# Two halves of an expert block's weighted sum moved earlier in a mixture-of-experts loop

## The chip, the cores and the metric

The kernel runs on one core of a Trainium2 chip. The metric is the device time of one execution in microseconds (us), as the median of several runs. TensorE (PE in the profile) multiplies matrices into PSUM, VectorE (DVE), ScalarE (ACT) and GpSimd (POOL) work element by element, SyncE (SP) issues the transfers from the chip's main memory, and each engine has an instruction queue of its own; semaphores tie them together.

## What is computed

A trunk of two layers over 256 tokens of width 1024. Each layer mixes tokens by three head groups side by side (windowed attention, a state space scan, latent attention) and then runs a mixture of 32 experts, of which each token takes two of one group of eight. The mixture is the part that matters here:

```
for g in range(N_EXPERT_GROUPS):
    h = silu(einsum('nd,edf->enf', xt, w_gate[g])) * einsum('nd,edf->enf', xt, w_up[g])
    h = h * gate[:, g].T[:, :, None]
    y = y + einsum('enf,efd->nd', h, w_down[g])
x = x + y
```

Every expert has three weight matrices of 1 MB (gate, up, down, each 1024 x 256 numbers of 4 bytes), so a layer's experts alone are 96 MB, which are read once.

## The kernel before

The function `moe` (L1194) walks over nine blocks per layer, seven of four experts and two of two. A block gives each of its experts an equal share of 128 slots: 32 with four experts, 64 with two. Its steps, with the names that the profile shows:

- **Weights.** All weights flow through a ring of 25 pages of 1 MB (tile `pg`). `pump` (L227) issues their transfers on SP in one fixed order; a page is taken again when the last instruction that reads it has run. Per block that is: first halves (`hf` 0) of gate and up of each expert, second halves (`hf` 1), then down.
- **Gather** (L1232, tile `gp`, copies into `xe`): one-hot matmuls pick the rows of the slots, in eight pieces k = 0 to 7. Two neighbouring blocks of four can share one gather. It is done one block ahead: the last block of such a group gathers for the next group, pieces 0 to 3 and then 4 to 7. The copies out of PSUM go to DVE and ACT in turn.
- **Gate and up** (`gate_up`, L1440, tile `gu`): 16 products per half with four experts, each recorded as two matmuls, 64 in all. In the last block of layer 1 the second half goes two experts at a time (L1447).
- **Hidden** (L1345): silu on ACT, a product on DVE. `hidden_t` (L1351, tile `hp`) turns it round on PE, and ACT copies it out.
- **Down** (L1459, tile `yp`): the product with the down weights; `split_y` (L1359) writes the sum as two parts, `yh` and `yl`.
- **Combine** (L1245, tiles `cp` and `x`): the block's sums go back to their tokens. It has two halves of 512 columns. One half is four matmuls (L1251, L1252: two for each 128 tokens) and two additions on DVE into `x` (L1253). It lies one block behind: the sums of a block (`pend`) are combined while the next block runs.

With four experts a slot share can overflow. Then a second pass runs under a condition that the chip evaluates: `tc.If(more > 0)` at L1568 (gather and first half of gate and up again) and at L1598 (second half, down and combine again). When it isn't needed, each engine waits there until its own earlier instructions are done, raises its semaphore by what it skips, and goes on. After one block of each layer (L1611) the pending sums are combined at once and the overflow of more than 64 tokens of an expert is handled (`units`, L1423); the block behind it has no `pend`.

The order in which a queue holds its instructions is not quite that of the source: the framework that lays the program out lets a later instruction pass one that is not ready by its own reckoning.

So in the source a block's order is: first half of gate and up, the condition of L1568, second half, hidden, [pieces 0 to 3 of the next gather], combine half 0, `hidden_t`, [pieces 4 to 7], combine half 1, the condition of L1598, down. The brackets are only in the last block of a gather group: blocks 0, 2, 3, 5, 7 of layer 0 and 0, 1, 2, 4, 5, 7 of layer 1, counted from 0.

Of the kernel before, what the change touches and what calls it, by code (L numbers as in the profile page):

```python
# [161 lines left out]
def hybrid_encoder_kernel(ctx, tc, I, out, dbg=None):  # L162
# [7 lines left out]
    def ps(name):  # L170
        return psp.tile([128, 512], F32, tag="ps", name=name)
# [83 lines left out]
    def page(*key):  # L255
        return st["tiles"][key]

    def done(*keys):
        for k in keys:
            del st["tiles"][k]  # L260
            st["ns"] -= 1
        pump()
# [931 lines left out]
    def moe(l, tab, rt):  # L1194
        with tc.tile_pool(name=f"moe{l}", bufs=1, reuse_waits="tile") as mo:
# [49 lines left out]
            def combine(pend, hfs=(0, 1)):  # L1245
                Sm, yh, yl = pend
                for hf in hfs:
                    for tt in range(2):
                        p = ps("cp")
                        c = slice(512 * hf, 512 * hf + 512)  # L1250
                        PE.matmul(p, Sm[:, 128 * tt:128 * tt + 128], yh[:, c], start=True, stop=False)  # L1251
                        PE.matmul(p, Sm[:, 128 * tt:128 * tt + 128], yl[:, c], start=False, stop=True)  # L1252
                        V.tensor_tensor(x[:, tt, c], p, x[:, tt, c], OP.add)  # L1253
# [186 lines left out]
            def gate_up(gu, blk, xs, hf, ahead=None):  # L1440

                m = 128 // len(blk)
                if ahead is not None:
                    for k in range(4 * hf, 4 * hf + 4):
                        ahead(k)

                two = end and blk == blks[-1] and hf == 1  # L1447
                for k, sp in [(k, s0) for s0 in range(0, len(blk), 2) for k in range(4 * hf, 4 * hf + 4)] if two else \
                        [(k, None) for k in range(4 * hf, 4 * hf + 4)]:
                    for s, e in list(enumerate(blk))[slice(sp, sp + 2) if two else slice(None)]:  # L1450
                        PE.matmul(gu[m * s:m * s + m, :].rearrange("p (a f) -> p a f", a=2), xs(k, s),  # L1451
                                  page(l, "gu", e, hf)[:, :, k % 4, :],
                                  start=(k == 0), stop=(k == 7), tile_position=(0, m * s))
# [51 lines left out]
            pend, scr = None, [None]  # L1505
# [8 lines left out]
            for g, grp in enumerate(groups):  # L1514
                if g < cut:
                    continue
                nb = len(grp)
                for ib, b in enumerate(grp):
                    blk, xe = blks[b], cur[1]
                    if b == UNIT_PREP[l] - 1:  # L1520
                        st["peak"] = 8
                    if b > 0:
                        scr[0] = work_page("scr")
                    if end and b == len(blks) - 1:
                        fin = [work_page(n) for n in ("fin", "yo")]
                        fg, xg = fin[0][:, :D], page_sm(fin[0], D, (2, 512))
                        yo = page_sm(fin[1], 0, (2, D))
                        nc.sync.dma_start(fg, I["final_g"].to_broadcast([128, D]))
                    if b == TAB_AT and tab is not None:
                        st["peak"] = 13  # L1530
                    m, o = 128 // len(blk), ib * len(blk)
                    if ib == nb - 1:
                        nxt = onehot(g + 1) if g + 1 < len(groups) else None
                        if nxt:
                            nxt[3](slice(0, 2))
                    gu, quad, w = ps("gu"), m == 32, {}
                    xs = lambda k, s: xe[:, k, o + s, :]
                    if b == 0:
                        ahead = lambda k: gather(cur[0], xe, k)
                        gate_up(gu, blk, xs, 0, ahead)  # L1540
                        if dbg and dbg.get("stop") == ("blk", l):
                            return
                        cn = counts()
                        if not quad:
                            done(*[(l, "gu", e, 0) for e in blk])
                        gate_up(gu, blk, xs, 1, ahead)
                        st["peak"] = 4
                        if not quad:
                            done(*[(l, "gu", e, 1) for e in blk])
                        scr[0] = work_page("scr")  # L1550
                        rt.gates()
                        pin(S.activation(mt([128, 1], "jka"), halfpi, AF.Silu))
                        uw["quad"] = quad_flags(cn)
                        pgt = weigh(cur[0], cur[2])
                    Sm, gs = fill_slots(slots([pgt[:, tt, o:o + len(blk), :].rearrange("p e c -> p (e c)")
                                               for tt in range(2)]))
                    if ib == nb - 1 and nxt:
                        pgt = weigh(nxt[0], nxt[2])
                    if quad:
                        if b > 0:  # L1560
                            gate_up(gu, blk, xs, 0)
                        f = blk[0] // 4
                        more = nc.values_load(uw["quad"][0:1, f:f + 1], min_val=0, max_val=1)
                        w = {"gu": ps("gu2"), "xs": page_sm(scr[0], 0, (8, 128)),
                             "P": scr[0][:, 1024:1280].rearrange("p (t e c) -> p t e c", t=2, e=4),
                             "S": slots(None, "2")[0]}
                        if b > 0:
                            with tc.If(more > 0):  # L1568
                                second(blk, w, 0)
                            done(*[(l, "gu", e, 0) for e in blk])  # L1570
                            gate_up(gu, blk, xs, 1)
                    elif b > 0:
                        for hf in range(2):
                            gate_up(gu, blk, xs, hf)
                            done(*[(l, "gu", e, hf) for e in blk])

                    hh = hidden(gu, gs)
                    for part in range(2):
                        if ib == nb - 1 and nxt:
                            for k in range(4 * part, 4 * part + 4):  # L1580
                                gather(nxt[0], nxt[1], k)
                        if pend is not None:
                            combine(pend, (part,))
                        if part == 0:
                            hT = hidden_t(hh)
                    if pend is not None:
                        work_done(1)
                    if b == 1:
                        uw["ui"], un = unit_list(cn)
                    y = w["y"] = y_page()  # L1590
                    if b == UNIT_PREP[l]:
                        unit_prepare()
                    if b == UNIT_AT[l]:
                        uw["y"] = y
                    if b > TAB_AT and tab is not None:
                        next(tab, None)
                    if quad:
                        with tc.If(more > 0):  # L1598
                            for hf in range(0 if b == 0 else 1, 2):
                                second(blk, w, hf)  # L1600
                        done(*[(l, "gu", e, hf) for hf in range(0 if b == 0 else 1, 2) for e in blk])
                    fn = final(Sm, *y) if end and b == len(blks) - 1 else None
                    pend = (Sm,) + down(blk, hT, y, next(fn) if fn else None)
                    if b == 0:
                        st["peak"] = 4
                    if b != UNIT_AT[l]:
                        work_done(1)
                    done(*[(l, "dn", e) for e in blk])
                    if b == 1:
                        uw["ub"] = unit_spread(un)  # L1610
                    if b == UNIT_AT[l]:  # L1611
                        combine(pend)
                        pend = None
                        n = 2 * MAXU
                        units(nc.values_load(uw["ui"][0:1, n:n + 1], min_val=0, max_val=MAXU))
                        work_done(6, 4)
                    if b >= TAB_AT and tab is not None:
                        next(tab, None)
                cur = nxt
# [86 lines left out]
```

## Time and profile before

| what | us |
|---|---|
| median of three runs | 730.94 |
| lowest and highest of them | 727.12, 731.55 |
| the profiled execution | 735.1 |
| its span, first to last instruction | 733.3 |
| PE busy in it | 639.2 |
| DVE busy | 373.2 |
| ACT busy | 252.9 |

In the profile a row of a timeline is a run of like instructions on an engine: start, duration, engine, source line, operation, tiles written and read, their shape and number, and in brackets how long the engine had been idle before and whose semaphore ended that. PEq or DVEq is an engine's instruction queue, where branches and semaphore instructions are carried out. A stage table gives for a stretch the busy time of each engine, the granted PE clock (1.00 is 2.4 GHz, 0.50 is 1.2 GHz), the share of time in which the 16 transfer engines were busy, and the rate in GB/s. Shares slightly over 1 come from how transfers are counted into a stretch.

### The profile page before, as it was taken

What the parts mean: (1) busy time and instruction counts of PE and PEld (TensorE: products, weight loads), DVE (VectorE), ACT (ScalarE), POOL (GpSimd) and SP (SyncE); (2) the same over time, 40 slices, a digit from 0 to 9 for tenths busy, and PEclk for the clock granted to TensorE, in tenths of its full rate; (3) what the DMA queues carried; (4) which work ended last, traced back from release to release, by engine and by line L of the source; (5) the groups of instructions that cost most, each with busy time, mean ns of one, the idle gap of its engine ahead of it and who ended that gap; (6) DMA issues with size and microseconds to landing.
All of it is one profiled execution on the core that took longest, in us unless ns stands there. A gap on an engine that the chain in (4) does not pass through costs nothing. (4 is left out here: it accounts for less than half of the span.)

```text
span 733.3 us, 12000 instructions
## 1 busy us (share of the span) xinstructions
PE 639.2 (87%) x4370; PEld 389.2 (53%) x4370; DVE 373.2 (51%) x899; ACT 252.9 (34%) x578; POOL 107.4 (15%) x135
## 2 busy tenths in 40 slices
PE   7997989988799797778899899999989978889994
PEld 6584877744245243326468777775534434334442
DVE  3899977532432228624369877762333323422424
ACT  3647764332111113444073397432202111011113
POOL 1202000100000022312032754500000000000001
PEclk9999999999899999789999899997999999999998
DMA  8920374895999999999996714796799999999991
GB/s 309 419 105 0 118 275 177 329 386 200 409 410 416 307 416 407 414 414 409 396 417 251 286 59 142 261 363 267 241 414 408 413 408 415 412 410 358 408 380 71
DMA packets 57201, 232.82 MB, mean 317 GB/s; under 512 B 6049, under 2 KB 8481, under 8 KB 48161
## 3 DMA queue, kind: packets, MB, share of 16 engines
q1 hardware_dynamic: 57120, 231.75, 81.3%
q8 instruction: 51, 0.84, 0.5%
q14 instruction: 30, 0.24, 0.1%
HBM read 233.82 MB, written 1.05 MB: 320 GB/s over the span
## 5 line engine op out<-in xcount | busy, mean ns | idle before, releaser
L1451 PE MATMUL gu<-pg,xe 128*32 128x512 f32 (+1 forms) x1024 | 149.5, 619 | 11.4 <-DMA pg<-in_w_up_dram 9.9
L1467 PE MATMUL yp<-pg,scr 128*32 128x512 f32 (+2 forms) x560 | 77.9, 628 | 26.1 <-DVEq L1598 12.8
L1451 PEld LDWEIGHTS gu<-pg,xe 128*32 128x32 f32 (+1 forms) x1024 | 45.9, 117 | 98.8 <-issue 94.5
L1236 PE MATMUL gp<-oh,xn 128*128 128x128 f32 (+1 forms) x416 | 73.6, 331 | 3.9 <-DVE oh L1221 1.6
L1236 PEld LDWEIGHTS gp<-oh,xn 128*128 128x128 f32 x416 | 62.9, 201 | 19.0 <-issue 11.3
L1467 PEld LDWEIGHTS yp<-pg,scr 128*32 128x32 f32 (+1 forms) x560 | 21.6, 119 | 72.1 <-issue 57.2
L1361 DVE TENSOR_TENSOR y<-yp,y 128x512 fp32r<-128x512 f32 (+1 forms) x39 | 26.3, 677 | 65.2 <-ACT y L1360 65.2
L1253 DVE TENSOR_TENSOR x<-cp,x 128x512 f32<-128x512 f32 x76 | 48.9, 684 | 19.0 <-PE cp L1252 19.0
L1228 POOL TENSOR_TENSOR pgt<-oh,gate 128x256 f32<-128x256 f32 (+1 forms) x13 | 10.2, 782 | 305.5 <-PE slp L372 294.3
L1348 DVE SCALAR_TENSOR_TENSOR scr<-gu,gs,scr 128x256 f32<-128x256 f32 x19 | 9.2, 482 | 89.9 <-ACT scr L1347 89.9
L1360 ACT CAST y<-yp 128x512 fp32r<-128x512 f32 (+1 forms) x39 | 22.3, 574 | 86.5 <-PE yp L1467 82.7
L359 DVE TENSOR_SCALAR xe<-gp,vec 128x128 f32<-128x128 f32 (+1 forms) x52 | 20.8, 400 | 54.6 <-PE gp L1236 54.6
L355 ACT ACTIVATE xe<-gp,vec 128x128 f32<-128x128 f32 (+1 forms) x52 | 21.1, 408 | 76.5 <-PE gp L1236 76.5
L1347 ACT ACTIVATE scr<-gu 128x256 f32<-128x256 f32 x19 | 7.3, 383 | 99.8 <-PEq L1568 50.9
L1251 PE MATMUL cp<-y,sm 128*128 128x512 f32 x76 | 33.5, 449 | 0.3 <-PEq L1568 0.2
L1252 PE MATMUL cp<-y,sm 128*128 128x512 f32 x76 | 29.9, 402 | 1.5 <-DVE y L1361 1.5
L1058 DVE SCALAR_TENSOR_TENSOR x<-op,rg,x 128x512 f32<-128x512 f32 x24 | 17.9, 748 | 16.9 <-PE op L681 11.9
L1341 ACT ACTIVATE scr<-slp 128x256 f32<-128x256 f32 x20 | 7.7, 387 | 35.4 <-PE slp L372 15.6
L1251 PEld LDWEIGHTS cp<-y,sm 128*128 128x128 f32 x76 | 14.3, 189 | 10.4 <-issue 8.2
L372 PE MATMUL hp<-cst,scr 128*128 128x128 f32 x40 | 9.2, 313 | 10.9 <-DVE scr L1348 9.8
L548 PE MATMUL t4p<-ca,tabs 128*32 128x32 f32 (+3 forms) x512 | 16.3, 250 | 2.1 <-issue 2.1
L548 PEld LDWEIGHTS t4p<-ca,tabs 128*32 128x32 f32 x512 | 15.4, 116 | 3.3 <-issue 3.0
(454 smaller groups left out, 1210.2 us busy)
## 6 DMA issues: line engine op xcount, KB each, us to landing
pg<-in_w_gate_dram SPq DMA_DIRECT2D x128, 512.0 KB, 10.2
pg<-in_w_up_dram SPq DMA_DIRECT2D x128, 512.0 KB, 10.2
pg<-in_w_down_dram SPq DMA_DIRECT2D x56, 1024.0 KB, 12.0
pg<-in_w_o_dram SPq DMA_DIRECT2D x8, 1024.0 KB, 17.9
pg<-in_w_down_dram SPq DMA_DIRECT2D x12, 512.0 KB, 10.4
pg<-in_w_qk_dram SPq DMA_DIRECT2D x4, 1024.0 KB, 14.9
pg<-in_w_nat_dram SPq DMA_DIRECT2D x4, 960.0 KB, 12.9
wgu<-in_w_gate_dram SPq DMA_DIRECT2D x4, 512.0 KB
```

Source lines behind the costliest of these rows:

```text
L355: S.copy(dst, src) if scale is None else S.activation(dst, src, AF.Copy, scale=scale)
L359: e.tensor_scalar(dst, src, scale, None, op0=OP.mult)
L548: PE.matmul(t4p[b][32 * jq:32 * jq + 32, c + lo:c + hi], g0[ri][:, 8 * d + i, :], ca[ri][:, 8 * d + i, m, :].rearrange("p m c -> p (m c)") ...
L1058: V.scalar_tensor_tensor(xh, p, rg[:, g, tt:tt + 1], xh, op0=OP.mult, op1=OP.add)
L1236: PE.matmul(p[:, :w], xn[:, tt, k, :], P[:, tt].rearrange("p e c -> p (e c)"), start=(tt == 0), stop=(tt == 1))
L1251: PE.matmul(p, Sm[:, 128 * tt:128 * tt + 128], yh[:, c], start=True, stop=False)
L1252: PE.matmul(p, Sm[:, 128 * tt:128 * tt + 128], yl[:, c], start=False, stop=True)
L1253: V.tensor_tensor(x[:, tt, c], p, x[:, tt, c], OP.add)
L1360: S.copy(yh[:, c], yp)
L1361: V.tensor_tensor(yl[:, c], yp, yh[:, c].bitcast(F32), OP.subtract)
L1451: PE.matmul(gu[m * s:m * s + m, :].rearrange("p (a f) -> p a f", a=2), xs(k, s), page(l, "gu", e, hf)[:, :, k % 4, :], start=(k == 0), sto ...
L1467: PE.matmul(yp[m * s:m * s + m, :], hT[:, j, m * s:m * s + m], page(l, "dn", e)[:, j, c], start=(j == 0), stop=(j == 1), tile_position=(0, ...
```

## The change

One half of `combine(pend)` leaves its place behind the hidden product and goes between the two halves of gate and up; the other half goes ahead of pieces 4 to 7 of the gather instead of behind them. No instruction is added or removed.

```diff
                             with tc.If(more > 0):
                                 second(blk, w, 0)
                             done(*[(l, "gu", e, 0) for e in blk])
+                            if pend is not None:
+                                combine(pend, (0,))
                             gate_up(gu, blk, xs, 1)
                     elif b > 0:
                         for hf in range(2):
+                            if hf and pend is not None:
+                                combine(pend, (0,))
                             gate_up(gu, blk, xs, hf)
                             done(*[(l, "gu", e, hf) for e in blk])
 
                     hh = hidden(gu, gs)
                     for part in range(2):
+                        if part == 1 and pend is not None:
+                            combine(pend, (1,))
                         if ib == nb - 1 and nxt:
                             for k in range(4 * part, 4 * part + 4):
                                 gather(nxt[0], nxt[1], k)
-                        if pend is not None:
-                            combine(pend, (part,))
                         if part == 0:
                             hT = hidden_t(hh)
                     if pend is not None:
```

## Rows read from the trace of the kernel before

**Rows 1.** The page, busy share of the transfer engines in 40 slices.
```profile
DMA  8920374895999999999996714796799999999991
```
**Rows 2.** Stage table: us; busy PE, PEld, DVE, ACT, POOL; clock; DMA share, GB/s.
```profile
256.00:370.00 114.00, 92.79 (x810) 44.85 (x806) 50.15 (x117) 35.88 (x69) 21.80 (x22) 0.91 1.03 410
...
519.00:598.00 79.00, 71.46 (x508) 35.19 (x502) 28.69 (x61) 13.92 (x36) 2.71 (x3) 1.00 1.02 399
598.00:620.00 22.00, 16.73 (x88) 9.43 (x86) 5.00 (x9) 2.65 (x6) 0.00 (x0) 1.00 1.02 415
...
685.60:717.70 32.10, 29.26 (x216) 15.02 (x215) 10.08 (x19) 5.44 (x15) 0.62 (x1) 1.00 0.97 364
```
**Rows 3.** PE timeline, end of layer 0: last down product, last sums.
```profile
369.74 1.90 PE L1467 MATMUL yp<-pg,scr 128*32 128x512 f32 x10 [0.27 <-DMA pg<-in_w_down_dram]
...
372.61 0.63 PE L1251 MATMUL cp<-y,sm 128*128 128x512 f32 x2
...
373.69 0.73 PE L1252 MATMUL cp<-y,sm 128*128 128x512 f32 x2 [0.16 <-DVE y L1361]
```
**Rows 4.** PE timeline, layer 1, block 5: its down product.
```profile
619.84 3.62 PE L1467 MATMUL yp<-pg,scr 128*32 128x512 f32 x26 [1.46 <-DMA pg<-in_w_down_dram]
```
**Rows 5.** PE timeline, layer 1, block 7 (with a gather), to its down product.
```profile
685.66 7.07 PE L1451 MATMUL gu<-pg,xe 128*32 128x512 f32 x64
692.92 2.02 PE L1236 MATMUL gp<-oh,xn 128*128 128x128 f32 x16 [0.18 <-PEq L1568]
694.70 0.48 PE L1251 MATMUL cp<-y,sm 128*128 128x512 f32 x1
...
695.72 0.39 PE L372 MATMUL hp<-cst,scr 128*128 128x128 f32 x2
...
698.43 0.40 PE L1252 MATMUL cp<-y,sm 128*128 128x512 f32 x1
700.00 3.64 PE L1467 MATMUL yp<-pg,scr 128*32 128x512 f32 x32 [1.17 <-DVEq L1598]
```
**Rows 6.** PE timeline, layer 1, block 8 (the last, no gather).
```profile
705.28 8.78 PE L1451 MATMUL gu<-pg,xe 128*32 128x512 f32 x62 [0.30 <-PEq L1568]
713.99 0.50 PE L1251 MATMUL cp<-y,sm 128*128 128x512 f32 x1
...
715.06 0.51 PE L372 MATMUL hp<-cst,scr 128*128 128x128 f32 x2
...
717.71 2.79 PE L1467 MATMUL yp<-pg,scr 128*32 128x512 f32 x32 [1.20 <-DVEq L1598]
```
**Rows 7.** Waits of PE over the whole span: us in total, times, longest.
```profile
PE yp L1467 <- DVEq L1598: 12.8, 9, 2.9
```
**Rows 8.** Timeline of ACT and DVE, layer 1, blocks 7 and 8.
```profile
697.93 0.37 ACT L355 ACTIVATE xe<-gp,vec 128x128 f32<-128x128 f32 x1 [0.53 <-PE gp L1236]
...
698.40 1.29 DVE L1253 TENSOR_TENSOR x<-cp,x 128x512 f32<-128x512 f32 x2 [0.56 <-PE cp L1252]
...
714.92 2.47 DVE L1253 TENSOR_TENSOR x<-cp,x 128x512 f32<-128x512 f32 x4
```
**Rows 9.** PE timeline, layer 1, block 1: gate and up ahead of L1568.
```profile
517.86 3.62 PE L1451 MATMUL gu<-pg,xe 128*32 128x512 f32 x26
```
**Rows 10.** SP timeline at that time: weight transfers issued.
```profile
519.10 0.33 SPq L247 DMA_DIRECT2D pg<-in_w_up_dram  x1
521.60 0.33 SPq L247 DMA_DIRECT2D pg<-in_w_gate_dram  x1
```
**Rows 11.** Granted clock: a stretch of layer 0, and 3.4 us in layer 1.
```profile
215.00:245.00 30.00, 26.72 (x138) 13.84 (x134) 10.95 (x19) 5.25 (x12) 1.05 (x1) 1.00 1.02 411
...
652.60:656.00 3.40, 3.40 (x19) 1.45 (x22) 0.34 (x1) 0.00 (x0) 0.00 (x0) 0.52 1.02 399
```
**Rows 12.** PE timeline, block 6 of layer 1: gate and up.
```profile
652.62 8.85 PE L1451 MATMUL gu<-pg,xe 128*32 128x512 f32 x64
```
**Rows 13.** PE timeline: a pause in that stretch of layer 0.
```profile
231.95 0.50 PE L372 MATMUL hp<-cst,scr 128*128 128x128 f32 x2 [1.64 <-DVE scr L1348]
```

## The prediction

> **What bounds the kernel now.** I read the page first. Its row for the transfer engines is full in two long stretches, the experts of layer 0 and of layer 1, and drops in between, where the second mixer computes and the ring of pages is full [rows 1]. The page's chain of waits breaks off at the condition of L1598 in the last block, so I went on with stage tables and followed the queues by hand. In layer 0 from 256 to 370 us the transfers are busy all the time (share 1.03, 410 GB/s), while PE is busy for 92.79 of 114 us; layer 1 is the same from 519 to 620 (share 1.02) [rows 2]. Who really waits is seen in the timeline at the end of such a stretch. The last down product of layer 0 stands still until a down page has landed, at 369.74 [rows 3], and that of block 5 in layer 1 until 619.84 [rows 4]. Up to these two points the weights set the pace, and whatever PE saves before them it spends as a longer wait for a page.
>
> Behind 619.84 it is the other way round. The overflow pass and the second pass of block 6 keep PE back, the pages are there, and PE with its waits on DVE and ACT is the path to the end. In that stretch PE is busy for 29.26 of 32.10 us from 685.6 to 717.7 [rows 2], and two of its waits belong to DVE's queue at L1598: 1.17 us in block 7 [rows 5] and 1.20 in block 8 [rows 6]. They are two of nine such waits, 12.8 us in all [rows 7]. Block 6 has no pending sums. So of the 14 blocks in which the change moves something (seven per layer), blocks 7 and 8 of layer 1 are those where it can reach the end.
>
> **What the wait at L1598 is.** In block 7, PE's last matmul of combine half 1 ends at 698.43 + 0.40 = 698.83 [rows 5]. DVE then still has the two additions, from 698.40 for 1.29 us, to 699.69 [rows 8]. Only when they are done does DVE raise its semaphore for the skipped pass, and down starts at 700.00, 0.31 us later [rows 5]. So a half of combine as the last work ahead of L1598 costs its additions, nearly 0.9 us behind PE's own end.
>
> **The change, part by part.** No instruction is added, so PE has the same matmuls. No DMA is issued by the moved step, and SP's issues keep their order, as `done` and `work_done` stay where they are; what shifts is when pages come free. The moved half now stands ahead of the second half of gate and up in PE's queue: 1.02 us for its four matmuls (694.70 to the next row at 695.72 [rows 5]). On DVE its additions would stand ahead of the hidden product, which needs the second half of gate and up anyway, and of nothing else that is late.
>
> *Block 7, with a gather.* Gate and up end 1.02 us later, and the rest of PE's work is 1.02 shorter. The hidden product stays covered by four pieces of gather (2.02 us [rows 5]). The order at the end is turned round: the additions of half 1 now run while pieces 4 to 7 do, and the last work ahead of L1598 is the copy of piece 7, 0.37 us on ACT [rows 8]. Put behind PE's end at 698.83 it ends at 699.20; with the same 0.31 us to the start of down that is 699.51 instead of 700.00: -0.5 us. Bounds: down cannot start before PE's own end and the 0.31 us, 699.14 (-0.9); and if the additions of 1.29 us push DVE's own copies back by as much, all is as before (0).
>
> *Block 8, without a gather.* Here the half that is moved had a use: with it PE filled the time of the hidden product. Gate and up end at 714.06, the turned product starts at 715.06 [rows 6], so hidden takes 1.00 us. The second half of gate and up runs without a wait for pages, so it ends 1.02 us later, at 715.08. What fills the 1.00 us then? By the source, nothing: `hidden_t` comes ahead of half 1. But a queue does not wait when something else is ready: at the end of layer 0 the matmuls of both 128-token groups on `yh` (L1251 x2) stand ahead of those on `yl`, which wait for DVE [rows 3], though the source has them the other way. So I expect half 1 to go into that gap. DVE then gets the hidden product at about 715.55 to 716.03 and two additions of 1.29 us, to 717.32, where four additions end at 714.92 + 2.47 = 717.39 today [rows 8]. Down starts 0.1 us earlier. Bounds: if the order of the source holds, `hidden_t` and half 1 behind it start 1.02 us later than today, and of this DVE, with two additions to do instead of four, gives back about 0.1: +0.9. If the moved matmuls fit into gate and up, which has a pause of 0.30 us at the condition and takes 8.78 us for 62 matmuls where block 7 takes 7.07 for 64 [rows 5, 6], the 1.02 us are saved as well: -1.1.
>
> *Before 619.84.* The moved half fills part of a wait for pages in the second half of gate and up, or delays the release of its pages by 1.02 us. I take 0: the transfers are full there, and PE waits for pages behind it. Bounds: rivals 1 and 2.
>
> **Sum.** -0.5 - 0.1 = -0.6 us; from the two pairs of bounds -2.0 to +0.9. The profiled execution took 735.1 us, 1.8 of it outside its span of 733.3, and would take 734.5. That is 4.2 us over the median of the runs, 730.94. Put on the median: **730.3 us**. The three runs of before spread from 3.8 below the median to 0.6 above, so a measurement of this kernel can tell about 1% (7.3 us) from no change, and this forecast lies inside it.
>
> **Rival 1, slower: a page comes free too late in block 1.** The pages of the first half of gate and up are released at L1568, since the second pass reads them too. In layer 1 that condition comes behind 26 of the 64 matmuls, at 521.5 [rows 9], and SP issues the next transfer at 521.60, 2.5 us after the one of 519.10 [rows 10]. Only four transfers of half a megabyte are then under way, 2 MB or about 5 us at 410 GB/s [rows 2], so the cover ends near 524. If the moved matmuls and the rest of gate and up come to stand ahead of the condition, it falls at about 521.5 + 4.2 (the other 38 at block 7's pace [rows 5]) + 1.0 = 527 and the transfers stand idle for nearly 4 us, which every later page inherits: +4 us, 734.3 with my -0.6. It decides from a delay of about 2 us on. Layer 0 starts in the same way, and both together make +8, 738.3. For it: in block 7 all 64 stand ahead of the condition [rows 5]. Against it: what holds the condition back need not move with PE's work. 0.16, of which 0.06 for both layers.
>
> **Rival 2, faster: PE counts in the full stretches too.** If pages came free earlier and the transfers took it up, each of the nine waits of 12.8 us [rows 7] would shrink, six of them by some 0.5 to 0.9 us: about -4 us, 726.9; at most, 0.31 us of each left, -10, 720.9. Against it: shares of 1.02 and 1.03 leave the transfers nothing to take up [rows 2]. 0.11, of which 0.04 beyond 7.3 us.
>
> **Rival 3, slower: the uncovered pause drops the clock.** PE ran 3.4 us at 0.52 behind the waits of the overflow pass [rows 11], and block 6's gate and up took 8.85 us there [rows 12] where block 7's took 7.07 [rows 5]: a price of 1.8 us. If the bare 1.00 us ahead of `hidden_t` did this in block 8, the sum would be +1.2: 732.1. The row against it: a pause of 1.64 us in layer 0 [rows 13] left the stretch around it at a granted clock of 1.00, the level of 2.4 GHz [rows 11]. 0.07. The Trainium skill, "TensorE: Matmul & The Clock Gate", section "HAM oscillation — how this bites in real kernels", speaks against a change like this one: an array that pauses between groups of matmuls is throttled again and starts each group slowly. By that rule block 8 would pay rival 3's price; the trace agrees for the long waits of the overflow pass and not for the pause of 1.64 us.
>
> **Rival 4: nothing moves.** The queues are laid out by readiness, and the halves could land where they are now, or DVE's copies take the time that its additions leave in block 7: 730.9. 0.08.
>
> **How the numbers follow.** The forecast has 0.58, with 728.9 to 731.8 as its own range from the bounds above. The range has to reach the one-layer case of rival 1 (734.3) and rival 2 (726.9), with the spread of the runs a little beyond: 726.5 to 734.8 leaves out the case of both layers and the far end of rival 2, 0.10, and some scatter. Faster by over 1% (under 723.6) is the far end of rival 2, 0.04; slower by over 1% (over 738.2) is rival 1 in both layers, 0.06; within 1% the rest, 0.90.
>
> **What would show it.** In blocks 7 and 8 of layer 1 four `cp` matmuls between two runs of `gu`; in block 7 the last PE work ahead of down is `gp`, and the wait on the queue at L1598 falls from 1.17 us to about 0.7; in block 8 `cp` stands between `gu` and `hp`, and down starts about 3.5 us after gate and up instead of 3.65. The last down product of layer 0 and that of block 5 in layer 1 still end a wait for a down page. I am wrong if those pages land at another distance from the start of the stream, if the transfers stand idle near 524 us, or if the stretch from 619.84 to the end changes by more than 2 us.

## The result: 0.5 to 0.9% slower, and the profile after

| what | us |
|---|---|
| changed kernel, median of 19 runs | 736.87 (733.02 to 741.05) |
| kernel before, 19 runs beside it | 730.94 (726.45 to 735.02) |
| ratio, 95% interval | 1.0088 (1.0069 to 1.0108), +5.0 to +7.9 us |
| the same comparison later (experiment 13) | 1.0050 (1.0023 to 1.0077), +1.7 to +5.6 us |
| profiled execution of the changed kernel, its span | 734.2, 732.4 |

I had forecast 730.3 and a range up to 734.8, so the forecast failed, sign included. The span of the profiled run is shorter than that of before although the kernel is slower: executions of one kernel differ by more than 8 us, and the two profiles are 6.1 us apart already at the first `gu` of block 1 of layer 0 (177.19 before, 171.08 after). Spans of single profiles are therefore not compared here; stages are.

First the waits of PE over the whole span of the changed kernel (us in total, times, longest):

```profile
PE hp L372 <- DVE scr L1348: 13.7, 9, 3.2
...
PE yp L1467 <- ACTq L1602: 9.0, 6, 4.8
PE yp L1467 <- DVEq L1602: 8.1, 5, 3.5
```

The same view of the kernel before, the two lines that were not shown:

```profile
PE hp L372 <- DVE scr L1348: 9.8, 6, 2.6
...
PE yp L1467 <- ACTq L1598: 4.7, 2, 4.2
```

The waits on DVE's queue at the second condition fall from 12.8 us [rows 7] to 8.1, as the change wants it. But ACT's queue takes their place, 4.7 to 9.0 us, so that the two together go from 17.5 to 17.1; and for the hidden product, whose time half 0 used to fill, PE now waits three times more (1.0 us each, in block 1 and in the last block of layer 0 and in the last block of layer 1) and 3.9 us longer in all.

Next the end of the kernel, PE's timeline of the changed kernel in blocks 7 and 8 of layer 1 (beside [rows 5, 6]):

```profile
683.76 7.08 PE L1451 MATMUL gu<-pg,xe 128*32 128x512 f32 x64
691.02 0.47 PE L1251 MATMUL cp<-y,sm 128*128 128x512 f32 x1 [0.18 <-PEq L1568]
...
694.97 1.95 PE L1236 MATMUL gp<-oh,xn 128*128 128x128 f32 x16
697.42 3.64 PE L1467 MATMUL yp<-pg,scr 128*32 128x512 f32 x32 [0.50 <-ACTq L1602]
...
702.71 3.92 PE L1451 MATMUL gu<-pg,xe 128*32 128x512 f32 x30 [0.30 <-DMA pg<-in_w_down_dram]
706.55 0.50 PE L1251 MATMUL cp<-y,sm 128*128 128x512 f32 x1
...
707.68 5.38 PE L1451 MATMUL gu<-pg,xe 128*32 128x512 f32 x32
714.07 0.50 PE L372 MATMUL hp<-cst,scr 128*128 128x128 f32 x2 [1.00 <-DVE scr L1348]
714.33 0.48 PE L1251 MATMUL cp<-y,sm 128*128 128x512 f32 x1
...
716.68 2.79 PE L1467 MATMUL yp<-pg,scr 128*32 128x512 f32 x32 [1.17 <-DVEq L1602]
```

Block 7 gains: the last work ahead of the condition is a gather, the wait is 0.50 us for ACT in place of 1.17 for DVE, and from the end of block 6's down to block 7's it takes 13.96 us in place of 14.64. Block 8 loses: half 0 lies between the halves of gate and up at 706.55, PE stands still for 1.00 us ahead of `hp`, and half 1 comes behind `hp`. From the end of block 7's down (701.06) to block 8's it takes 15.62 us in place of 14.07. Block 8 of layer 0 does the same. PE's timeline of the changed kernel there:

```profile
351.98 1.91 PE L1451 MATMUL gu<-pg,xe 128*32 128x512 f32 x12 [1.58 <-DMA pg<-in_w_up_dram]
354.19 0.47 PE L1251 MATMUL cp<-y,sm 128*128 128x512 f32 x1 [0.30 <-PEq L1568]
...
355.27 1.92 PE L1451 MATMUL gu<-pg,xe 128*32 128x512 f32 x14
358.21 0.51 PE L372 MATMUL hp<-cst,scr 128*128 128x128 f32 x2 [1.01 <-DVE scr L1348]
...
360.81 5.26 PE L1467 MATMUL yp<-pg,scr 128*32 128x512 f32 x32 [1.17 <-DVEq L1602]
```

And that of the kernel before:

```profile
359.08 3.98 PE L1451 MATMUL gu<-pg,xe 128*32 128x512 f32 x26 [1.04 <-DMA pg<-in_w_up_dram]
...
364.06 0.50 PE L372 MATMUL hp<-cst,scr 128*128 128x128 f32 x2
...
366.70 2.77 PE L1467 MATMUL yp<-pg,scr 128*32 128x512 f32 x22 [1.20 <-DVEq L1598]
```

From the arrival of that gate and up page to down it is 8.83 us in place of 7.62. The last wait for a down page that I had leaned on [rows 3] is gone: `yp` runs all 32 without one. Whether the 1.2 us are lost is seen at the end of down. Before, the pages stretch the product: it runs from 366.70 to 371.64 [rows 3], 4.94 us at a granted clock of 1.00, and ends 12.56 us behind the arrival. In a second profile of the changed kernel (experiment 12) it takes 3.74 us, at 1.00 as well, and ends 12.57 us behind the arrival, so nothing is lost. PE's timeline of experiment 12:

```profile
363.87 3.74 PE L1467 MATMUL yp<-pg,scr 128*32 128x512 f32 x32 [1.17 <-DVEq L1602]
```

In the first profile the same product takes 5.26 us, at a granted clock of 0.69 on average, and ends 14.09 us behind the arrival: what is lost there, 1.5 us, is the clock.

The largest piece lies in block 1 of layer 1. PE's timeline of the changed kernel:

```profile
512.53 4.83 PE L1451 MATMUL gu<-pg,xe 128*32 128x512 f32 x32
517.29 0.50 PE L1251 MATMUL cp<-y,sm 128*128 128x512 f32 x1
...
525.05 1.95 PE L1236 MATMUL gp<-oh,xn 128*128 128x128 f32 x16
530.51 5.34 PE L1467 MATMUL yp<-pg,scr 128*32 128x512 f32 x32 [3.50 <-DVEq L1602]
```

The down product of the same block before:

```profile
534.85 3.64 PE L1467 MATMUL yp<-pg,scr 128*32 128x512 f32 x32 [2.86 <-DVEq L1598]
```

Before, this is 16.99 us behind the block's first `gu` (517.86 [rows 9]), now 17.98. DVE is what ends last. It works out the list of overflow units here (lines 1305 to 1320), and in the changed kernel the last of that and the next one-hot stand ahead of the condition. DVE's timeline, changed kernel:

```profile
528.80 0.61 DVE L1317 TENSOR_REDUCE un<-uo 1x7 f32<-1x448 f32 x1
529.45 0.16 DVE L1320 CAST ui<-un 1x15 int32<-1x15 f32 x1
529.53 0.67 DVE L1221 TENSOR_TENSOR oh<-cst,rk 128x512 f32<-128x512 f32 x1
```

Kernel before, where both are behind it:

```profile
533.93 0.61 DVE L1317 TENSOR_REDUCE un<-uo 1x7 f32<-1x448 f32 x1
534.75 0.16 DVE L1320 CAST ui<-un 1x15 int32<-1x15 f32 x1 [0.21 <-DVEq L1598]
534.84 0.67 DVE L1221 TENSOR_TENSOR oh<-cst,rk 128x512 f32<-128x512 f32 x1
```

Behind the pause `yp` takes 5.34 us in place of 3.64. The stage table of the changed kernel (columns as in [rows 2]) has the clock in that product, and the transfers 35 us later:

```profile
532.00:534.00 2.00, 2.00 (x16) 0.64 (x12) 0.00 (x0) 0.56 (x1) 0.00 (x0) 0.50 1.08 440
...
556.00:570.00 14.00, 12.65 (x94) 4.59 (x94) 4.71 (x8) 2.31 (x6) 0.00 (x0) 1.00 0.95 370
566.00:568.00 2.00, 1.82 (x12) 1.32 (x9) 1.30 (x3) 0.54 (x2) 0.00 (x0) 1.00 0.55 143
...
683.70:716.60 32.90, 29.83 (x216) 13.99 (x214) 10.16 (x19) 5.34 (x15) 0.62 (x1) 1.00 0.88 330
```

The kernel before, the same two stretches:

```profile
534.80:538.50 3.70, 3.65 (x33) 1.20 (x33) 1.40 (x3) 0.58 (x1) 0.00 (x0) 1.00 1.02 407
...
556.00:570.00 14.00, 13.82 (x95) 5.21 (x94) 4.69 (x10) 2.42 (x7) 0.00 (x0) 1.00 1.03 410
```

The granted clock was 0.50 (1.2 GHz) in the product, 1.00 before. At 566 us the transfers stand idle for nearly half of 2 us, where before they were full. (The last line, blocks 7 and 8, answers to the last of [rows 2].) SP's timeline of the changed kernel says why:

```profile
552.82 0.33 SPq L247 DMA_DIRECT2D pg<-in_w_up_dram  x1
558.78 0.33 SPq L247 DMA_DIRECT2D pg<-in_w_gate_dram  x1
559.15 0.43 SPq L247 DMA_DIRECT2D pg<-in_w_up_dram  x1
559.75 0.33 SPq L247 DMA_DIRECT2D pg<-in_w_down_dram  x1
...
566.28 1.29 SPq L247 DMA_DIRECT2D pg<-in_w_down_dram  x3
```

And SP's waits from 553 to 567 us (us in total, times, longest):

```profile
SPq L247 <- PEq L1568: 4.9, 1, 4.9
SPq L247 <- PE yp L1467: 4.7, 1, 4.7
```

With all pages taken, SP issues nothing for 6.0 us, until 558.78: block 2's down ends at 558.75 and frees pages. After three issues it stops again, from 559.75 to 566.28: the next pages come free when PE has passed the first condition of block 3, L1568. Both places come as late as PE is. Before, the two gaps were 2.2 us (558.69 to 560.92) and 5.9 us (562.57 to 568.42). In the end block 5's last down page, the one of [rows 4], lands 104.19 us behind block 1's first `gu` (616.72) and not 101.98. Its products then run slowly as well, 5.29 us in place of 3.62, at 0.67 on average, which no other trace shows. PE's timeline of the changed kernel:

```profile
616.72 5.29 PE L1467 MATMUL yp<-pg,scr 128*32 128x512 f32 x26 [1.47 <-DMA pg<-in_w_down_dram]
```

### The profile page after: what moved, and what is told of

It is laid out like the page before. It is cut to its first block, busy times and chain, and to the rows that moved or that the text cites. A ratio compares the mean times of both kernels' runs of the same rounds, so it can differ in the third digit from the quotient of the medians.

```text
span 732.4 us, 12008 instructions
## 1 busy us (share of the span) xinstructions
PE 638.2 (87%) x4370; PEld 382.1 (52%) x4370; DVE 374.9 (51%) x899; ACT 252.5 (34%) x578; POOL 107.9 (15%) x135
## 5 line engine op out<-in xcount | busy, mean ns | idle before, releaser
L1451 PE MATMUL gu<-pg,xe 128*32 128x512 f32 (+1 forms) x1024 | 152.0, 617 | 10.5 <-DMA pg<-in_w_up_dram 9.9
L1467 PE MATMUL yp<-pg,scr 128*32 128x512 f32 (+2 forms) x560 | 79.5, 646 | 25.0 <-ACTq L1602 9.0
L1451 PEld LDWEIGHTS gu<-pg,xe 128*32 128x32 f32 (+1 forms) x1024 | 42.9, 116 | 99.3 <-issue 93.2
L1236 PE MATMUL gp<-oh,xn 128*128 128x128 f32 (+1 forms) x416 | 71.5, 325 | 3.1 <-DVE oh L1221 1.6
L1236 PEld LDWEIGHTS gp<-oh,xn 128*128 128x128 f32 x416 | 62.8, 198 | 14.3 <-issue 5.9
L1251 PEld LDWEIGHTS cp<-y,sm 128*128 128x128 f32 x76 | 14.3, 190 | 19.7 <-issue 17.7
L372 PEld LDWEIGHTS hp<-cst,scr 128*128 128x128 f32 x40 | 6.5, 204 | 23.0 <-DVE scr L1348 16.2
L1252 PEld LDWEIGHTS cp<-y,sm 128*128 128x128 f32 x76 | 14.0, 189 | 5.3 <-DVE y L1361 3.8
```

Source lines behind the costliest of these rows:

```text
L372: PE.transpose(dst, src, ident[:src.shape[0], :src.shape[0]])
L1236: PE.matmul(p[:, :w], xn[:, tt, k, :], P[:, tt].rearrange("p e c -> p (e c)"), start=(tt == 0), stop=(tt == 1))
L1467: PE.matmul(yp[m * s:m * s + m, :], hT[:, j, m * s:m * s + m], page(l, "dn", e)[:, j, c], start=(j == 0), stop=(j == 1), tile_position=(0, ...
```

## The experiments

**Theory A**: three places lose (block 8 of either layer, and block 1 of layer 1 through DVE's chain, the clock and late pages) and block 7 of layer 1 gains. **Theory B**: nearly all is lost in the last block. **Theory C**: the loss is spread over all blocks or lies elsewhere. In every kernel two switches choose the blocks with the new places:

```diff
+E0 = lambda b: ...; E1 = lambda b: ...
-if pend is not None:
+if pend is not None and E0(b):
     combine(pend, (0,))
...
-if part == 1 and pend is not None:
+if part == 1 and pend is not None and E1(b):
     combine(pend, (1,))
 if ib == nb - 1 and nxt:
     ...
+if pend is not None and not (E0, E1)[part](b):
+    combine(pend, (part,))
```

All stages that were read, from the timelines of PE, one line a kernel, in us: (a) block 8 of layer 0, from the arrival of the gate and up page to down; (b) block 1 of layer 1, wait ahead of down; (c) its 32 down products; (d) from its first `gu` to the end of block 5's down; (e) end of block 6's down to block 7's; (f) end of block 7's down to block 8's.

```
                               a      b     c      d       e      f
before                        7.62  2.86  3.64  105.60  14.64  14.07
11 before again               7.62  2.86  3.64  105.48  14.63  14.07
after                         8.83  3.50  5.34  109.48  13.96  15.62
12 after again                8.83  3.50  4.92  108.33  13.96  15.61
13 after, third time          8.84  3.50  4.92  107.98  13.95  15.62
1  after, b1 old              8.86  2.86  3.64  106.04  13.95  15.61
2  after, b8 old             10.38  3.50  5.34  108.01  13.95  14.08
3  before, b1 new             7.63  3.50  5.34  108.16  14.62  14.08
4  before, b8 new             7.62  2.86  5.34  106.05  14.63  15.54
5  after, three old           7.62  2.86  5.34  108.77  13.97  14.07
6  before, late list          7.63  1.17  3.64  106.36  14.61  14.07
7  after, late list           8.85  0.56  3.64  105.80  13.95  15.55
8  two old, late list         7.63  0.56  3.64  106.24  13.98  14.07
9  half 1, late list          7.63  0.56  3.64  106.94  13.95  13.92
10 half 0                     8.84  2.86  5.24  107.17  14.68  15.55
14 layer 0 new                8.85  2.86  5.34  106.26  14.63  14.08
15 layer 1 new                7.63  3.57  5.22  108.03  13.95  15.54
```

**1 to 4: one block back, one block alone.**

```diff
1: +E0 = E1 = lambda b: not (l == 1 and b == 1)
2: +E0 = E1 = lambda b: not (l == 1 and b == 8)
3: +E0 = E1 = lambda b: l == 1 and b == 1
4: +E0 = E1 = lambda b: l == 1 and b == 8
```

> The changed kernel with the old places in block 1 of layer 1 alone; every other block keeps the new ones. The two traces put about +3.9 us of the loss between block 1 and block 5 of layer 1: in block 1 the products yp start 1.0 us later after the block's first gu (17.98 against 16.99), run at half the granted clock (5.34 us against 3.64), pages come free later, and the transfers then stand idle about 2.3 us near 566 us. Theory A (block 1 starts all of this): about 733.0 us, ratio to the kernel before about 1.003, the wait ahead of yp back to 2.9 us, no idle transfers near 566 us. Theory B (the loss is in the last block, which lost the work that covered it): about 736.9 us, ratio 1.008. Theory C (the loss is spread over all blocks, or lies in layer 0): within 1 us of the changed kernel, 736 to 737 us.

> The changed kernel with the old places in the last block (block 8 of layer 1) alone. Theory A (block 1 of layer 1 carries 3.9 us, the last block 1.5 us): about 735.4 us, ratio about 1.006. Theory B (the last block carries most): 731 to 732 us, ratio about 1.001. Theory C (spread or layer 0): about 736.5 us, ratio 1.008. In the profile, from the end of block 7's yp to the start of block 8's yp: 17.7 us by A and B, 19.3 us by C.

> The kernel before with the new places in block 1 of layer 1 alone, the other direction of the first run. Theory A: about 734.8 us, ratio about 1.005, with the wait ahead of yp at 3.5 us and the transfers idle near the place where the changed kernel's were. Theory B: about 731 us, ratio 1.000. Theory C: about 731.5 us, ratio 1.001, since one block of 16 carries a sixteenth.

> The kernel before with the new places in the last block alone, the other direction of the second run. Theory A: about 732.4 us, ratio 1.002, and 19.3 us from the end of block 7's yp to the start of block 8's yp in place of 17.7. Theory B: 735 to 736 us, ratio 1.006. Theory C: about 731.3 us, ratio 1.0005.

Measured against before: 1.0046 (1.0015 to 1.0077), 1.0031 (1.0001 to 1.0061), 1.0024 (0.9992 to 1.0055), 1.0024 (0.9995 to 1.0053). The intervals are too wide for one run to decide, but both blocks count and neither is all: B falls, as its ratios lie outside the intervals of 1 and 4. C as a loss spread over all blocks lies outside that of 2; a loss elsewhere stays open until 13 to 15. The stages are sharper. Block 8 costs 1.5 us wherever it has the new places (column f). Block 1 lengthens (d) by 2 to 3 us in 2 and 3, not in 1. (In the expectations of 2 and 4 the 17.7 and 19.3 us are counted from the start of block 7's `yp`, 3.6 us ahead of column f.) One miss: in 4 block 1 is as before, with the same 2.86 us of waiting, and yet its products ran slowly. PE's timeline of experiment 4:

```profile
525.11 5.34 PE L1467 MATMUL yp<-pg,scr 128*32 128x512 f32 x32 [2.86 <-DVEq L1604]
```

So the clock can fall there with the old places too, and of its 1.7 us all but 0.5 were then absorbed before the end of block 5 (106.05).

**5 to 8: three blocks back; DVE's list moved.** The list goes from block 1 of layer 1 to the start of block 2, where DVE is idle for 7 us.

```diff
5: +E0 = E1 = lambda b: (l, b) not in ((0, 8), (1, 1), (1, 8))
6: +E0 = E1 = lambda b: False
7: +E0 = E1 = lambda b: True
8: +E0 = E1 = lambda b: (l, b) not in ((0, 8), (1, 8))
6, 7, 8:
+if b == 2 and l == 1:
+    uw["ui"], un = unit_list(cn)
...
-if b == 1:
+if b == 1 and l == 0:
     uw["ui"], un = unit_list(cn)
...
-if b == 1:
+if b == 1 + l:
     uw["ub"] = unit_spread(un)
```

> The changed kernel with the old places in three blocks: the last block of layer 0, and blocks 1 and 8 of layer 1. By the stages of the six traces so far these three carry the whole loss (block 8 of layer 0 +1.2 us from the arrival of its last page to yp, block 1 of layer 1 +2.6 us up to the end of block 5, block 8 of layer 1 +1.5 us), and block 7 of layer 1 gains 0.67 us. Theory A (three places): 0.7 us below the kernel before, about 729.7 us, ratio 0.999. Rival C (the other twelve blocks carry a part): 732 to 733 us, ratio 1.003 or more.

> The kernel before, with the list of overflow units (the operations of lines 1305 to 1320) computed at the start of block 2 of layer 1 in place of block 1; sums and gathers as before. It takes some 3 us of VectorE's work from the chain ahead of block 1's condition. Theory A: yp of block 1 starts 14.3 to 14.8 us after the block's first gu in place of 17.0, at the full granted clock; the transfers were never idle there, so the end moves by 0 to -0.5 us: ratio 0.999 to 1.000. Rival (TensorE's time in block 1 goes to the end one for one): -2.5 us, ratio 0.9965.

> The changed kernel with the list of overflow units at the start of block 2 of layer 1. Theory A (block 1 costs because VectorE's chain with the list ends later, TensorE pauses and runs at half clock, and the pages come free too late): from the first gu of block 1 to the end of block 5 106.0 us in place of 109.5, no transfers idle near 566 us, and about 734.3 us, ratio 1.0045. Rival (half 0 ahead of the second half costs there by its place alone): 109 us and 736.9 us, ratio 1.0088.

> The version by which the experiments would beat both: the new places in all blocks but the last of either layer, and the list of overflow units at the start of block 2 of layer 1. Theory A: block 7 gains 0.67 us and nothing else moves, 729.5 us, ratio 0.9985. Rival C (the new places cost in the other blocks too): 732 us, ratio 1.002.

Measured: 1.0014 (0.9985 to 1.0043), 0.9979 (0.9950 to 1.0009), 1.0021 (0.9995 to 1.0047), 0.9995 (0.9963 to 1.0028). The intervals of 5 and 8 hold the ratios of both A and C, so the stages have to decide. Experiment 7 settles block 1: with the new places kept and only the list moved, (d) is 105.80, and the clock does not fall in block 1. PE's timeline of experiment 7:

```profile
528.66 3.64 PE L1467 MATMUL yp<-pg,scr 128*32 128x512 f32 x32 [0.56 <-DMA pg<-in_w_gate_dram]
```

Its stage table has no idle transfers:

```profile
550.00:580.00 30.00, 27.66 (x193) 11.05 (x194) 9.53 (x17) 5.04 (x13) 0.61 (x1) 1.00 1.02 412
```

But the list's price went along to block 2. There DVE makes the one-hot of the next gather behind the list. PE's timeline of experiment 7, block 2:

```profile
543.94 5.41 PE L1236 MATMUL gp<-oh,xn 128*128 128x256 f32 x16 [2.98 <-DVE oh L1221]
```

PE waits 2.98 us, and the 16 matmuls run at a granted clock of 0.68 (5.41 us; 3.72 in block 2 before). So block 2's down starts only 0.9 us later than before, counted from block 1's first `gu`: PE's lateness there is small, and the transfers stay full although the clock fell.

In 6 `yp` of block 1 starts 15.30 us behind the first `gu`, later than the 14.3 to 14.8 expected, and this earlier start is not seen in (d): 106.36. Block 2 waits for the one-hot as in 7. Its ratio points to a gain but reaches past 1, so neither of the two expectations is shown. Experiment 5 missed in one point: block 1 was old, its clock fell as in 4, and this time the transfers did stand idle. Stage table of experiment 5:

```profile
568.00:572.00 4.00, 3.46 (x22) 1.69 (x14) 2.41 (x5) 0.76 (x2) 0.00 (x0) 1.00 0.68 229
```

What goes with the loss in all traces is how late block 2's down starts, counted from block 1's first `gu` (39.4 us before): +1.7 us in 4 and 14, where (d) is 106.1 and 106.3; +2.4 in 10 (107.2); +2.7 to +2.8 in 3, 12 and 13 (108.0 to 108.3); +3.1 to +3.2 in 2, 15 and the changed kernel (108.0, 108.0 and 109.5, of which 1.7 is block 5's own slow down product); +3.9 here (108.8). From about 2 us on the transfers feel it. With the late list it is +0.9 at most, and no transfers stand idle near that place; (d) is 105.8 to 106.9 there, which shows its scatter.

**9 and 10: the two parts of the change apart.**

```diff
9:  +E0 = lambda b: False; E1 = lambda b: True   (and the late list)
10: +E0 = lambda b: True; E1 = lambda b: False
```

> Only the second half of the change (half 1 of the sums ahead of gather pieces 4 to 7), half 0 in its old place everywhere, and the list of overflow units at the start of block 2 of layer 1. Theory A: half 1 alone brings the gain of block 7 (from the end of block 6's yp to the start of block 7's yp 13.96 us in place of 14.64), half 0 alone brings the losses, so nothing is lost here: the last blocks as before (14.07 us from block 7's yp to block 8's), and about 729 to 729.5 us, ratio 0.997 to 0.998. Rival (half 0 behind the last gate and up products brings the gain, half 1 nothing): 14.6 us ahead of block 7's yp, ratio 0.999 or more.

> Only the first half of the change (half 0 of the sums ahead of the second half of gate and up), half 1 in its old place everywhere, and the list of overflow units in its old place. Theory A: it carries all losses (block 8 of layer 0 +1.3, block 8 of layer 1 +1.5, block 1 of layer 1 about +2) and none of the gain: about 735.5 us, ratio 1.006 to 1.008, 14.6 us ahead of block 7's yp and 15.6 us ahead of block 8's. Rival (the two halves lose together, half 1 in block 1 above all): 733 us, ratio 1.003.

Measured: 1.0001 (0.9974 to 1.0027) and 1.0036 (1.0010 to 1.0061). Half 1 alone brings the gain of block 7 (13.95) and loses nothing in the last blocks. Half 0 alone brings both delays there (8.84, 15.55) and no gain (14.68); its ratio is the lower end of what A expected and fits the rival's 1.003 too. In block 1 half 0 alone leaves the wait at 2.86 us; half 1 alone with the list in its old place was not tried.

**11 and 12: both kernels once more**, one profile each.

> The kernel before, unchanged, for a second profile of it. In four traces with the old places in block 1 of layer 1 the wait ahead of its yp was 2.86 us and yp took 3.64 us in two and 5.34 us in two. If the granted clock falls there by chance in the kernel before, this trace shows either; if it falls only where other blocks have new places, 3.64 us. With 5.34 us the stretch from the first gu of block 1 to the end of block 5 should be longer than 105.6 us.

> The changed kernel, unchanged, for a second profile of it. By theory A the longer wait (3.50 us) makes the granted clock fall every time: yp of block 1 of layer 1 takes 5.34 us again, and the stretch to the end of block 5 takes 108 to 110 us. If the fall is chance alone, 3.64 us and 106 to 107 us.

732.16 and 733.44 us; the stages repeat within 0.1 us but for (c) and (d). With a wait of 2.86 us and the list in block 1, `yp` ran at the full clock in three kernels (before, 11, 1) and slowly in four (4, 5, 10, 14); with 3.50 or 3.57 us slowly in six of six; with 0.56 to 1.17 us (the late list) at full clock in four of four.

The last block of layer 0 has its own count, from the arrival of the page to the end of down. With the old places (nine traces) it is 12.53 to 12.75 us, and 13.40 in 5, with a granted clock of 1.00 in every down product. With the new ones, and the bare pause of 1.01 us, it is 12.56 to 12.63 us in 1, 7, 12 and 14, where the down product ran at 1.00, and 14.09, 14.17, 14.15 and 15.49 us in the first profile, 13, 10 and 2, where it ran at 0.68 to 0.70. So column (a) shows a delay of 1.2 us that the wait for pages takes up; lost are 0 or 1.5 us (2.9 in 2, where the clock had fallen in gate and up already), 0.8 as the mean of the eight against the nine.

**13 to 15: what the stages leave over.** Up to here they gave +3.7 us of 6.4.

```diff
13: +E0 = E1 = lambda b: True
14: +E0 = E1 = lambda b: l == 0
15: +E0 = E1 = lambda b: l == 1
```

> The changed kernel, unchanged, timed again beside the next two. If the stages hold the whole loss, 3.7 us above the kernel before, ratio 1.005; if some 2.7 us more lie where no stage was read, 6.4 us, ratio 1.0088 as at first.

> The change in layer 0 alone, layer 1 with the old places. By the stages +1.0 us, ratio 1.0014. If the missing part lies in layer 0 (or in the clock of the mixer behind it), +2.5 to +3.7 us, ratio 1.0035 to 1.005.

> The change in layer 1 alone, layer 0 with the old places. By the stages +2.7 us (block 1 to 5 +1.8, block 7 -0.67, block 8 +1.54), ratio 1.0037. If the missing part lies in layer 1, +4 to +5.4 us, ratio 1.0055 to 1.0075.

Measured: 1.0050 (1.0023 to 1.0077), 1.0019 (0.9996 to 1.0043), 1.0021 (1.0000 to 1.0041). 15 leaves no room for the missing part in layer 1; for layer 0 the interval of 14 still holds the lowest case, 1.0035. From the traces: the last block of layer 0 +0.8; (d) 108.3 as the mean of the six traces with both halves new in block 1 and the list there, against 106.4 of the six with the old places and the list, +2.0; (e) -0.7; (f) +1.5: together **+3.6 us**. With each kernel's own (d), (e) and (f) against 106.4, 14.6 and 14.1, and 0.8 where the last block of layer 0 is new, the sum lies inside the interval of every experiment that was timed, 13 included; the first comparison begins at +5.0. The traces have no place for the rest. From block 1's first `gu` in layer 1 to the end of the program it is 215.4 and 215.2 us before and 219.9, 218.5 and 218.3 in the changed kernel; from block 1's first `gu` in layer 0 to that point 340.7 and 340.9 against 341.5, 339.1 and 339.7. That is +1.6 to +5.2 us, as in the second comparison; why the first gave more stays open. Part of it can be the clock: in 13 the two slowest executions (739.08 and 739.26 us) have the low mean granted clocks 0.943 and 0.947, the two fastest (731.06 and 731.08 us) 0.958. No version was shown to be faster than the kernel before: 8 and 9 were meant to be and are at 0.9995 and 1.0001.

## Why the prediction was wrong

- **Block 7: right.** Forecast -0.5 us, measured -0.68, by the step that was named: the additions run beside the last gather pieces, and ACT's copy comes last. Half 0 stood behind all 64 `gu` and the first condition, not between the halves, but that did no harm.
- **Block 8: the step "I expect half 1 to go into that gap" failed.** Half 1 stayed behind `hp`, so the order of the source held, for which I had a bound of +0.9. "A queue does not wait when something else is ready" is not what happened: PE stood still for 1.00 us with half 1 next behind `hp` in its queue and the sums ready. [rows 3] show how the queue was laid out, not that it reorders while it runs. The bound measured +1.5, as two of its terms were off. Gate and up end later by more than the 1.02 us of half 0: 12.00 us behind block 7's down in place of 10.42, as its two halves now run apart (3.92 and 5.38 us for 62 matmuls, 9.30 in place of 8.78 [rows 6]); that they overlapped before is the likely reason, not a tested one. And behind them 3.62 us pass to down in place of 3.65: DVE, with half the additions, gave back 0.03 us and not 0.1.
- **"Before 619.84: I take 0" failed, twice.** In layer 0 the pages did take up the delay: 1.2 us of it, all that they stretched the down product by (4.94 us before, 3.74 in experiment 12). The row that I read, 0.27 us [rows 3], is only a part of that slack, and I had not counted it. What failed there is the clock, which I had priced for block 8 of layer 1 alone: 1.5 us or more in four of eight traces. In layer 1 the page itself came later (by 2.2 us in the first profile), since PE's lateness in block 1 held back pages. That is the largest term, +2.0 us, and I had put it at 0.
- **Rival 1 had the mechanism and missed the place.** Pages freed too late did leave the transfers idle, but near 566 us and not 524. The first condition of block 1, L1568, stood behind 32 `gu` in place of 26 and did no harm; block 2's down and the first condition of block 3 came too late. That the 2 us from which it was to decide were about right is luck, as they were worked out for another place. Its price was also added wrongly: from 524 to 527 is 3 us and not nearly 4. I looked for the place where the change reorders PE's queue; the trigger was DVE's queue. The longest of the nine waits, 2.9 us [rows 7], was in block 1, and I never asked what DVE did in it.
- **Rival 3 had the clock and missed the places.** The bare pause of 1.00 us in block 8 of layer 1 left the clock at 1.00 (683.70 to 716.60 in the stage table), as the 1.64 us of [rows 13] had. The same bare pause in the last block of layer 0, and the wait of 1.17 us behind it, were followed by a low clock in four of eight traces, for 1.5 us or more; the 3.50 us in block 1 of layer 1 were followed by 0.50. The section cited there from the Trainium skill ("TensorE: Matmul & The Clock Gate", section "HAM oscillation — how this bites in real kernels") speaks of long waits between groups of matmuls, after which each group starts slowly. The trace agrees in block 1, where the wait is 3.50 us. A pause as short as the 1.00 us of block 8 is not its case, though I had applied it there, and it does not tell of the falls behind 1.01 and 1.17 us in layer 0.
- **Sum and range.** A late page, an uncovered hidden product and a fallen clock each stood in the text, as a bound or in a rival, but as cases that exclude each other. They came together: 4.3 us of cost beside 0.7 of gain.

What is shown: that block 1 and block 8 of layer 1 lose and by how much (1 to 5, 15), that the list in DVE's queue ahead of block 1's condition is needed for block 1's loss (7), that half 0 is the part that costs in the last blocks (9, 10), and that the last block of layer 0 lost only where the clock fell. Argued only: that the bare pause brings the clock down there (four of eight traces with it, none of nine without); that PE's lateness at block 2's down is what empties the transfers (it goes with the loss in every trace, and was not changed by itself); and how the 0.6 us by which block 1's wait is longer split between the cast and the one-hot ahead of the condition, since that order was not undone alone.

## What to carry to other kernels

Ahead of a change, ask of each piece of work which wait it fills where it stands now: a matmul that covers a chain through two other engines is worth more than the place that it takes up. "The transfers bound this stretch" holds only as far as the slack that the rows show; write it down in microseconds for each place where pages come free, over the whole product that waits and not one row of it, and compare. Work that is moved out of one wait can make another: behind the list of overflow units PE waited 2.86 us in block 1, and 2.98 us in block 2 once it was moved there. And where an order is planned by a program, a moved instruction can push another engine's work across a condition, so read every queue there, not only the one that was edited.

## What was not expected of the hardware

The same wait of 2.86 us ahead of the same 32 matmuls was followed by 3.64 us at full clock in three executions and by 5.24 to 5.34 us in four. What a kernel's own timeline shows at such a place is one draw; it took seven profiles to see that both are usual there. The last block of layer 0 is the same: behind pauses of 1.01 us and 1.17 us, between which PE works for 1.4 us, the same 32 matmuls took 3.71 to 3.77 us in four executions and 5.11 to 5.33 us in four.
